# A transformer step whose second feed-forward runs its first w2 blocks as plain products, with earlier operand fetches and a norm in whole pieces

## The chip, the cores and the metric

The kernel runs on one NeuronCore of a Trainium2 chip. The metric is the device time of one execution in microseconds (us). Five engines work side by side: TensorE (PE, matrix products), VectorE (DVE), ScalarE (ACT), GpSimd (POOL) and SyncE (SP). SP and POOL issue most of the DMAs here, each from a queue of its own that goes out in order.

## The reference

One layer of a diffusion trunk on 640 tokens (512 latent, 128 context), width 1024: a SwiGLU feed-forward at half weight, token mixing (attention beside an mLSTM), and a second feed-forward at half weight. The part that is changed most is the second feed-forward, with the norm ahead of it:

```python
def swiglu(h, w1, w3, w2):
    return (jax.nn.silu(h @ w1) * (h @ w3)) @ w2
...
    hh = rmsnorm(x, g[2]) * (1 + m[7]) + m[6]
    x = x + 0.5 * m[8] * swiglu(hh, p['ffn2_w1'][l], p['ffn2_w3'][l], p['ffn2_w2'][l])
```

w1 and w3 are 1024 x 2816, w2 is 2816 x 1024. m[6] to m[8] are shift, scale and gate from the conditioning vector, one column per feature and kind of token.

## The kernel before

**Precision.** Each fp32 operand is held as a high part (rounded to fp32r) and a low part (the rest, also fp32r), and each product is three matmuls: high by high, high by low, low by high. To split something is therefore an ACT copy into the high part, and a DVE subtract for the low part. Weights that are split whole are called ww (a pair of 128x2048 tiles); those of some products come in smaller tiles wB and wC.

**Layout.** Features lie on partitions, tokens on the free axis; tokens come in two halves (hf) of 320, features of x in 8 tiles of 128 (KT), two of them to a pair. A matmul is 128x128 weights by 128x320.

**Up.** The 2816 hidden features are 11 blocks (FB) of 256. Block 0 is computed plainly from W, by 8 steps over k for the two output tiles f and both of w1, w3 (`plain`, L312). For each of the other ten blocks a granule (`Granule`, L230) holds 256 columns of w1, and another those of w3. Its product (2 x 2 in output tiles and token halves, two halves of the inner axis) goes through a scheme of Strassen's kind with seven products instead of eight: A11, S1, S2, A12, S3, A22, S4 (`products`, L378). The A are plain parts of the operands, the S sums of parts. For the weights, `parts` (L243) copies and splits the parts A11, A12 (wB) and S4 (wC), and then forms the sums in place in the raw tile; `sums` (L261) splits these into ww. For the tokens, `operand_sums` (L328) forms S1, S3, S2, S4 from the normed x, with a high part by ACT and a low part by DVE, into tiles S and hm. A granule's own A22 and S4 products (`tail`) run a granule later, between the next one's.

**Between.** silu and product give four quarters of a block in tile SO; `gated_sums` (L358) adds the four sums for down's scheme, and `store_g` (L346) splits 7 pieces into tiles g and writes them to g_dram on SP's queue.

**Down.** In the second half-step (`run`, L539) the 11 blocks form the groups 0-2, 3-6 and 7-10. For each group and each of four column blocks (j) of 256 outputs, a granule of w2 goes through the same seven products, with operands fetched from g_dram into the tiles of earlier operands (`fetch`, L553, on POOL's queue): each fetch is issued when TensorE has ended the last product that reads its tile, in the last granule before the group. In the first half-step (`run_whole`, L487) all groups of down are plain products with weights split whole (`Whole`, L270).

**Norm.** `normed` (L1774) takes one half of the tokens: for each feature tile and kind of token, DVE multiplies x by scale and 1/rms in one operation (L42), ACT writes the high part with the shift as its bias (L1788), DVE makes the low part. A pass on ACT later adds the shift to x itself (L1820), which the operand sums read. For the second half, the pieces are 192 and 128 tokens wide, since it holds latent and context tokens.

**Order.** TensorE and the loads (`dma`) keep the program's order. On the other engines and for the rest of SP's queue a list scheduler sets the order at build time from modelled times; `issue_after(ins)` ties what follows behind an instruction on the same engine.

Of the kernel before, what the change touches and what calls it, by code (L numbers as in the profile page):

```python
# [7 lines left out]
F32 = mybir.dt.float32  # L8
# [10 lines left out]
NS = 512  # L19
# [12 lines left out]
def tile_trunk(ctx: ExitStack, tc: tile.TileContext, a: dict):  # L32
# [197 lines left out]
    class Granule:  # L230
# [5 lines left out]
        def load(self):  # L236
            self.raw = rawp.tile([128, 2048], F32, tag="raw", name="raw")[:, : 512 * self.nk].rearrange("p (k n) -> p k n", n=256)
            self.fetch(self.raw)
# [22 lines left out]
        def sums(self):  # L261
# [4 lines left out]
            tt(vec, t[1], flat, t[0].bitcast(F32), ALU.subtract)  # L266
# [26 lines left out]
    class HalfStep:  # L293
        def __init__(self, n, fp, tmp, psum, w1, w3, w2, whole=False):

            self.whole, self.n_g = whole, 4 if whole else 8
            self.Q = {(kh, hf): kh + 2 * hf for kh in range(2) for hf in range(2)} if whole else Q
# [4 lines left out]
            self.g_dram = dp.tile([4 if whole else 7, 128, 2, FB, HALF], F32, name=f"g_dram{n}")  # L302
# [14 lines left out]
        def begin_gated(self):  # L317
            self.SO = self.fp.tile([128, 8, HALF], F32, tag="SO", name="SO")[:, : self.n_g]
# [9 lines left out]
        def operand_sums(self, pair):  # L328
# [6 lines left out]
            for i, to, x, y, op in (  # L335
                (S1, (1, 1), (0, 1), (1, 1), ALU.add), (S3, (0, 1), (0, 0), (0, 1), ALU.subtract),
                (S2, (0, 0), (1, 1), (0, 0), ALU.subtract), (S4, (1, 0), (1, 0), (0, 0), ALU.subtract),
            ):
                for r in range(2):
                    v, x_, y_ = (a[r][kh][hf] for kh, hf in (to, x, y))  # L340
                    ks = slice(2 * r, 2 * r + 2)
                    tt(vec, v, x_, y_, op)
                    act(SS[i][:, 0, ks], v, AF.Copy)
                    tt(vec, SS[i][:, 1, ks], v, SS[i][:, 0, ks].bitcast(F32), ALU.subtract)

        def store_g(self, SO, b):  # L346

            if not self.whole:
                self.gated_sums(SO)
            for tag, c0, c1 in (("gA", 0, 4), ("gB", 4, 7)):  # L350
                if c0 < self.n_g:
# [26 lines left out]
        def products(self, work, between, then=(), behind=None):  # L378
# [72 lines left out]
        def up_done(self, b):  # L451
# [10 lines left out]
            def of_w3(f, hf, p, u):  # L462
                if (f, hf) == (0, 0):
                    self.begin_gated()
# [9 lines left out]
        def fetch_w2(self, b0, b1, j):  # L474
            def f(raw):
                n = b1 - b0
                for h in range(2):
                    dma(raw[:, h * n : (h + 1) * n], self.w2[b0:b1, :, h, 256 * j : 256 * j + 256].rearrange("b p n -> p b n"))
# [60 lines left out]
        def run(self, x, gate, final, between, emptied=lambda: None, behind=None):  # L539


            work = self.up_work()

            at = {(0, i): self.ops[i] for i in range(7)}
            moves = {}
            for q, places in ((1, (None, None, 0, 1, 2, 3, 4)), (2, ((0, 5), 0, 1, (0, 6), 3, 4, 2))):
                for i, j in enumerate(places):
                    if j is not None:
                        before = j if type(j) is tuple else (q - 1, j)
                        at[q, i] = at.get(before)  # L550
                        moves[before] = q, i

            def fetch(q, i):  # L553
                b0, b1 = GROUPS[q]
# [1402 lines left out]
```

## Time and profile before

| | before |
|---|---|
| median of 3 runs | 1887.62 us (1882.26 to 1888.84) |
| profiled execution | 1888.76 us |
| its span | 1886.9 us |
| mean granted TensorE clock | 0.984 |
| DVE, ACT busy | 70%, 45% of the span |

A row of the timeline gives start, duration, engine, line, operation, output<-inputs, shapes and count, and in brackets how long the engine had been idle before and what ended it. A list of waits gives the total, the number and the longest. A row of a table of windows gives the window, then for PE, PEld, DVE, ACT and POOL busy us and count, then the granted clock, the share in which the DMA engines were busy, and GB/s. A group of instructions has its count, busy us, mean ns of one, and the idle time before it. A row on DMA issues has the count, KB of each and the median us from issue to landing. In the span the first half-step's feed-forward begins at about 40 us, the second's at 1443, its down part at 1730.

### The profile page before, as it was taken

The page shows a single profiled execution, that of the slowest core. Times are in us where ns is not written, and L with a number is a line of the kernel's source. Part 1 is how long each engine was busy: PE and PEld are TensorE (multiplying, and loading weights), DVE is VectorE, ACT ScalarE, POOL GpSimd, SP SyncE. Part 2 cuts the span into 40 slices and gives each one's busy share as a digit, 9 for nine tenths or more (in the row PEclk, how much of TensorE's full clock was granted, in tenths as well). Part 3 has the DMA queues.
Part 4 walks back from the last instruction along what each step waited for, and adds up shares of the span by engine and source line. Part 5 has one row for each costly group of instructions (what it writes and reads, how often), then busy time and mean ns, then how long its engine had stood idle before and what let it go on. Part 6 is the DMA issues. An engine that isn't in the chain of part 4 may idle for free.

```text
span 1886.9 us, 30810 instructions
## 1 busy us (share of the span) xinstructions
PE 1812.6 (96%) x12622; PEld 1774.3 (94%) x12622; DVE 1329.4 (70%) x2252; ACT 854.6 (45%) x1469; POOL 45.9 (2%) x71
## 2 busy tenths in 40 slices
PE   5899999999999999999999989999999999998989
PEld 4899999999999999999999979999999899998989
DVE  6888896577885675865755447864458888886775
ACT  5554444112454354543554445564325555553332
POOL 1000001010000000000000000000000000001100
PEclk8899999999999999999999999999999999999999
DMA  8344557964413323322222255564532455457962
GB/s 326 105 151 173 186 175 267 374 206 140 137 63 129 121 74 104 111 95 84 95 84 75 72 174 157 190 245 145 198 114 77 172 187 187 172 180 271 355 219 91
DMA packets 129614, 305.72 MB, mean 162 GB/s; under 512 B 9601, under 2 KB 93057, under 8 KB 116673
## 3 DMA queue, kind: packets, MB, share of 16 engines
q1 hardware_dynamic: 117298, 247.33, 38.1%
q0 software_dynamic: 12176, 56.43, 7.9%
q8 instruction: 99, 1.62, 0.4%
q14 instruction: 41, 0.34, 0.1%
HBM read 237.15 MB, written 66.58 MB: 161 GB/s over the span
## 4 chain that ended last, share of the span: by engine, by line
PE 82%; DVE 8%; DMA 6%; ACT 2%; issue 1%; SPq 0%; DVEq 0%; ACTq 0%
PE ps_f L52 36%; PE ps_p L52 22%; PE ps_t L52 12%; PE sc L52 2%; PE ps_o L52 2%; PE ps_n L52 2%; DMA raw<-in_w2b 2%; DMA ada<-csil_dram 2%; DVE ww L39 1%; PE ps_u L52 1%; PE ps_wT L55 1%; PE ps_qkT L55 1%; DVE x L42 1%; DVE raw L39 1%; DMA raw_a<-in_w_ada_c 0%
## 5 line engine op out<-in xcount | busy, mean ns | idle before, releaser
L52 PE MATMUL ps_f<-S,ww 128*128 128x320 f32 x2052 | 332.2, 311 | 5.6 <-DVE S L39 4.2
L52 PEld LDWEIGHTS ps_f<-S,ww 128*128 128x128 f32 x2052 | 309.9, 189 | 8.3 <-DVE S L39 4.7
L52 PE MATMUL ps_p<-hH,wH 128*128 128x320 f32 x864 | 274.1, 317 | 3.3 <-ACT aT L1275 2.5
L52 PE MATMUL ps_p<-hH,wL 128*128 128x320 f32 x864 | 267.5, 310 | 0.0
L52 PE MATMUL ps_p<-hL,wH 128*128 128x320 f32 x864 | 267.3, 309 | 0.0
L52 PE MATMUL ps_t<-wH,hH 128*128 128x256 f32 x640 | 186.3, 291 | 1.0 <-DVE x L42 1.0
L52 PE MATMUL ps_f<-hm,wB 128*128 128x320 f32 x1128 | 182.5, 311 | 0.0
L52 PE MATMUL ps_t<-wH,hL 128*128 128x256 f32 x640 | 182.4, 285 | 0.0
L52 PE MATMUL ps_t<-wL,hH 128*128 128x256 f32 x640 | 182.1, 285 | 0.0
L52 PEld LDWEIGHTS ps_f<-hm,wB 128*128 128x128 f32 x1128 | 170.9, 189 | 0.0
L52 PE MATMUL ps_f<-hm,ww 128*128 128x320 f32 x996 | 158.0, 311 | 11.7 <-ACT u L375 9.5
L52 PEld LDWEIGHTS ps_p<-hH,wH 128*128 128x128 f32 x864 | 162.9, 189 | 4.8 <-ACT aT L1275 2.7
L39 DVE TENSOR_TENSOR ww<-raw,ww 128x2048 fp32r<-128x2048 f32 (+1 forms) x62 | 138.7, 2237 | 35.6 <-ACT ww L265 23.4
L52 PEld LDWEIGHTS ps_p<-hL,wH 128*128 128x128 f32 x864 | 163.0, 189 | 0.5
L52 PEld LDWEIGHTS ps_p<-hH,wL 128*128 128x128 f32 x864 | 162.6, 188 | 0.0
L52 PEld LDWEIGHTS ps_f<-hm,ww 128*128 128x128 f32 x996 | 149.8, 189 | 12.5 <-ACT u L375 10.1
L39 DVE TENSOR_TENSOR wL<-raw,wH 128x2048 fp32r<-128x2048 f32 x49 | 112.1, 2289 | 40.0 <-ACT wH L123 39.9
L39 DVE TENSOR_TENSOR raw<-raw 128x1024 f32<-128x1024 f32 (+2 forms) x156 | 132.7, 851 | 2.1
L123 ACT ACTIVATE wH<-raw 128x2048 fp32r<-128x2048 f32 x49 | 93.6, 1911 | 87.5 <-PE ps_p L52 83.3
L265 ACT ACTIVATE ww<-raw 128x2048 fp32r<-128x2048 f32 (+1 forms) x52 | 97.8, 1880 | 73.2 <-PE ps_f L52 51.7
L52 PEld LDWEIGHTS ps_t<-wH,hH 128*128 128x128 f32 x640 | 123.7, 193 | 2.0 <-issue 1.2
L52 PEld LDWEIGHTS ps_t<-wH,hL 128*128 128x128 f32 x640 | 123.7, 193 | 0.5 <-DVE hL L42 0.5
(294 smaller groups left out, 3288.1 us busy)
## 6 DMA issues: line engine op xcount, KB each, us to landing
g_dram<-g SPq DMA_DIRECT2D x44, 640.0 KB, 4.2
raw_a<-in_w_ada_c SPq DMA_DIRECT2D x24, 512.0 KB, 4.1
hm<-g_dram POOLq DMA_DIRECT2D x9, 1280.0 KB, 12.9
raw<-in_w1b SPq DMA_DIRECT2D x11, 1024.0 KB, 4.8
raw<-in_w3b SPq DMA_DIRECT2D x11, 1024.0 KB, 4.8
g_dram<-g SPq DMA_DIRECT2D x22, 480.0 KB, 4.6
raw<-in_w1a SPq DMA_DIRECT2D x10, 1024.0 KB, 4.9
raw<-in_w3a SPq DMA_DIRECT2D x10, 1024.0 KB, 5.9
```

The source lines that it names most:

```text
L39: return eng.tensor_tensor(out=out, in0=in0, in1=in1, op=op)
L42: return vec.scalar_tensor_tensor(out=out, in0=in0, scalar=scalar, in1=in1, op0=op0, op1=op1)
L52: tc.keep_in_program_order(nc.tensor.matmul(*args, **kw))
L55: tc.keep_in_program_order(nc.tensor.transpose(*args, **kw))
L123: act(h, raw, AF.Copy)
L265: act(t[0], flat, AF.Copy)
```

## The change

Four parts of the program are changed.

1. Down's first group of the second half-step (blocks 0-2) becomes plain: no gated sums for these blocks, four stored pieces, weights split whole.
2. Its operands are fetched on SP's queue as the last up granule ends with each of A11, S1, S2, A12; those of the second group during the plain stage, placed behind weight loads; two of the third group's on SP behind the load of the second group's last granule, the other five on POOL in that granule.
3. The norm multiplies by 1/rms in DVE operations over a pair of tiles, ACT applies scale and shift twice (into the high part L1838 and into x itself L1839), and the low part is one DVE subtract a pair. The shift pass is gone.
4. The operand sums stand in an order written out by hand, and a granule's parts are tied behind the split of the granule before it (of the first granule in the second half-step: behind the low part of S2). `products` and `operand_sums` serve both half-steps.

```diff
-    GROUPS = ((0, 3), (3, 7), (7, FB))
+    GROUPS = ((3, 7), (7, FB))
+    PLAIN_Q = {(kh, hf): kh + 2 * hf for kh in range(2) for hf in range(2)}
...
-            tt(vec, t[1], flat, t[0].bitcast(F32), ALU.subtract)
+            self.split_at = tt(vec, t[1], flat, t[0].bitcast(F32), ALU.subtract).ins
...
-        def begin_gated(self):
-            self.SO = self.fp.tile([128, 8, HALF], F32, tag="SO", name="SO")[:, : self.n_g]
+        def begin_gated(self, b):
+            self.Q, n = (PLAIN_Q, 4) if b < self.n_plain else (Q, 8)
+            self.SO = self.fp.tile([128, 8, HALF], F32, tag="SO", name="SO")[:, :n]
...
+            for f, i, r in (
+                (terms, S1, 0), (terms, S1, 1), (terms, S3, 0), (low, S1, 0), (terms, S2, 0), (low, S1, 1), (terms, S3, 1),
+                (terms, S2, 1), (low, S2, 0), (low, S2, 1), (low, S3, 0), (low, S3, 1), (terms, S4, 0), (terms, S4, 1),
             ):
-                for r in range(2):
-                    v, x_, y_ = (a[r][kh][hf] for kh, hf in (to, x, y))
-                    ks = slice(2 * r, 2 * r + 2)
-                    tt(vec, v, x_, y_, op)
-                    act(SS[i][:, 0, ks], v, AF.Copy)
-                    tt(vec, SS[i][:, 1, ks], v, SS[i][:, 0, ks].bitcast(F32), ALU.subtract)
+                f(i, r)
+                if (f, i) == (low, S2):
+                    behind = prev.ins
+            low(S4, 0)
+            low(S4, 1)
+            return behind
 
         def store_g(self, SO, b):
 
-            if not self.whole:
+            n = 4
+            if b >= self.n_plain:
                 self.gated_sums(SO)
+                n = 7
...
-            work[0][0].parts(self.fp)
-            work[0][0].sums()
+            if not prepared:
+                work[0][0].parts(self.fp)
+                work[0][0].sums()
...
                 if not last:
-                    with ExitStack() as st:
-                        if i == 0 and behind is not None:
-                            st.enter_context(tc.issue_after(behind))
+                    with tc.issue_after(behind if i == 0 and behind is not None else gr.split_at):
                         work[i + 1][0].parts(self.fp)
...
-        def run(self, x, gate, final, between, emptied=lambda: None, behind=None):
+        def run(self, x, gate, final, behind=None):
...
+            n = self.n_plain
+            down = [Whole(n, self.fetch_w2(0, n, j)) for j in range(4)]
+
+            up = self.ops
+            at = [[up[i] for i in (A11, S1, S2, A12)], [up[i] for i in (S3, S4, A22)], None]
+
+            def fetch(q, i, eng=nc.sync):
+                b0, b1 = ((0, n), *GROUPS)[q]
+                eng.dma_start(out=at[q][i][:, :, : b1 - b0].bitcast(F32), in_=self.g_dram[i, :, :, b0:b1, :])
...
-            def fetch(q, i):
-                b0, b1 = GROUPS[q]
-                nc.gpsimd.dma_start(out=at[q, i][:, :, : b1 - b0].bitcast(F32), in_=self.g_dram[i, :, :, b0:b1, :])
...
+            work[-1][3] = lambda i: {A11: lambda: fetch(0, 0), S1: lambda: fetch(0, 1), S2: lambda: fetch(0, 2), A12: lambda: fetch(0, 3)}.get(i, nothing)()
+            self.products(work, nothing, down[:2], behind=behind)
+            at[1] += [self.fp.tile([128, 2, 4, HALF], F32R, tag=tag, name="op") for tag in ("gA", "SO")] + at[0][:2]
...
                 def used(i):
-                    if j == 3 and (q, i) in moves:
-                        fetch(*moves[q, i])
+                    if q == 1 and j == 3 and i in moves:
+                        fetch(2, moves[i], nc.gpsimd)
...
+            moves = {A11: S2, S1: A12, S2: S3, A12: A22, S3: S4}
+            for j in range(4):
+                ahead = down[j + 2] if j < 2 else last[j - 2][0]
+                loaded = ahead.load()
+                with tc.issue_after(loaded):
+                    for i in ((A11, S1), (S2, A12), (S3,), ())[j]:
+                        fetch(1, i)
+                if j < 3:
+                    down[j + 1].split()
+                else:
+                    last[0][0].parts(self.fp)
+                    last[0][0].sums()
+                for hf in range(2):
+                    for f in range(2):
+                        p = acc_tile(self.psum)
+                        for kh in range(2):
+                            op = at[0][PLAIN_Q[kh, hf]]
+                            for b in range(n):
+                                w = [down[j].w(i, n * kh + b, f) for i in range(2)]
+                                mm3(p, *w, op[:, 0, b], op[:, 1, b], kh + b == 0, kh == 1 and b == n - 1)
+                        add_residual(x, p, 2 * j + f, hf, gate)
+                    if (j, hf) == (3, 0):
+                        for i in (A22, S4):
+                            fetch(1, i, nc.gpsimd)
+
+            def load_last(load=last[3][0].load):
+                with tc.issue_after(load()):
+                    for i in (A11, S1):
+                        fetch(2, i)
+
+            last[3][0].load = load_last
+            self.products(last, nothing, prepared=True)
...
-        for d in range(KT):
-            for s0, s1, j in SEGS[hf]:
-                xs = x[d][:, s0:s1]
-                h, lo = (t[:, s0 - c0 : s1 - c0] for t in hs.hh(d, hf))
-                sh = shift[:, d, j : j + 1]
-                stt(xs, xs, scale[:, 2, d, j : j + 1], rs[:, s0 - c0 : s1 - c0], ALU.mult, ALU.mult)
-                act(h, xs, AF.Identity, bias=sh)
-                ins = stt(lo, xs, sh, h.bitcast(F32), ALU.add, ALU.subtract)
-        return ins.ins
+        for g in range(4):
+            xs = x_pairs[g][:, :, half(hf)]
+            tt(vec, xs, xs, rs[:, None, :].to_broadcast([128, 2, HALF]), ALU.mult)
+            for d in (2 * g, 2 * g + 1):
+                for s0, s1, j in SEGS[hf]:
+                    by = dict(scale=scale[:, 2, d, j : j + 1], bias=shift[:, d, j : j + 1])
+                    act(hs.hh(d, hf)[0][:, s0 - c0 : s1 - c0], x[d][:, s0:s1], AF.Identity, **by)
+                    act(x[d][:, s0:s1], x[d][:, s0:s1], AF.Identity, **by)
+            p = hs.part[g // 2, hf][:, :, 2 * (g % 2) : 2 * (g % 2) + 2]
+            tt(vec, p[:, 1], xs, p[:, 0].bitcast(F32), ALU.subtract)
...
-    for d in range(KT):
-        for s0, s1, j in ((0, NS, 0), (NS, T, 1)):
-            xs = x[d][:, s0:s1]
-            act(xs, xs, AF.Identity, bias=m_of(6)[:, d, j : j + 1])
-    hs.operand_sums(lambda r: x_pairs[r])
+    summed = hs.operand_sums(lambda r: x_pairs[r])
```

What this does to the order. First, TensorE where down begins; hm and S are operand tiles, ww, wB, wC weights. Before, one column block of the group:

```order
L52 MATMUL ps_f<-hm,wB 128x320 x9
L52 MATMUL ps_f<-S,ww 128x320 x9
L52 MATMUL ps_f<-hm,ww 128x320 x9
L52 MATMUL ps_f<-S,ww 128x320 x9
L52 MATMUL ps_f<-hm,wC 128x320 x9
L52 MATMUL ps_f<-hm,wB 128x320 x9
L52 MATMUL ps_f<-S,ww 128x320 x9
```

and now, where the rows of one column block are 9, 9, 9, 18, 9, 9 and 9 with the last and first of neighbours joined:

```order
L52 MATMUL ps_f<-hm,ww 128x320 x18
L52 MATMUL ps_f<-S,ww 128x320 x9
L52 MATMUL ps_f<-hm,ww 128x320 x9
L52 MATMUL ps_f<-S,ww 128x320 x18
L52 MATMUL ps_f<-hm,ww 128x320 x9
L52 MATMUL ps_f<-S,ww 128x320 x9
```

A column block has 72 matmuls instead of 63, all with whole split weights, on four operands instead of seven.

Second, SP's queue at the same place, from the first loads of w2 on (L74; raw is a weight tile, hm, S and op are operand tiles). Before:

```order
L74 DMA raw<-in_w2b 128x3x256 x4
L356 DMA g_dram_14354<-g 128x4x320
L356 DMA g_dram_14354<-g 128x3x320
L356 DMA g_dram_14354<-g 128x4x320
L356 DMA g_dram_14354<-g 128x3x320
L74 DMA raw<-in_w2b 128x3x256 x4
L356 DMA g_dram_14354<-g 128x4x320
L356 DMA g_dram_14354<-g 128x3x320
L356 DMA g_dram_14354<-g 128x4x320
L356 DMA g_dram_14354<-g 128x3x320
L74 DMA raw<-in_w2b 128x4x256 x16
```

and now, from behind the first loads and two stores:

```order
L581 DMA hm<-g_dram_14354 128x2x960
L384 DMA g_dram_14354<-g 128x4x320
L384 DMA g_dram_14354<-g 128x3x320
L581 DMA S<-g_dram_14354 128x2x960 x2
L74 DMA raw<-in_w2b 128x3x256 x2
L581 DMA hm<-g_dram_14354 128x2x960
L581 DMA S<-g_dram_14354 128x2x1280
L581 DMA hm<-g_dram_14354 128x2x1280
L384 DMA g_dram_14354<-g 128x4x320
L74 DMA raw<-in_w2b 128x3x256 x2
L581 DMA hm<-g_dram_14354 128x2x1280
```

The fetches (L581), which were all on POOL's queue, now stand between the loads and the stores. POOL keeps seven of 128x2x1280.

Third, ACT at the norm of the second half of the tokens (s is the silu of block 0). Before, the end of the norm and the shift pass:

```order
L1788 ACTIVATE hm<-x,mod 128x128
L1788 ACTIVATE hm<-x,mod 128x192
L1820 ACTIVATE x<-x,mod 128x512
L1788 ACTIVATE hm<-x,mod 128x128
L1820 ACTIVATE x<-x,mod 128x128
L1820 ACTIVATE x<-x,mod 128x512
L1820 ACTIVATE x<-x,mod 128x128
L325 ACT_TABLE_LOAD
L325 ACTIVATE s<-ps_f 128x320
```

and now:

```order
L1839 ACTIVATE x<-x,mod,scale 128x192
L1839 ACTIVATE x<-x,mod,scale 128x128
L1838 ACTIVATE hm<-x,mod,scale 128x128
L1839 ACTIVATE x<-x,mod,scale 128x192
L327 ACT_TABLE_LOAD
L327 ACTIVATE s<-ps_f 128x320
L1839 ACTIVATE x<-x,mod,scale 128x128
L1839 ACTIVATE x<-x,mod,scale 128x192
L1839 ACTIVATE x<-x,mod,scale 128x128
L327 ACTIVATE s<-ps_f 128x320
```

The last operations on x, which the low parts of the last two pairs now read, stand behind the table load and a silu.

Fourth, DVE amid the first half-step's norm (mod, small and scale belong to the modulation). Before, with the second granule's parts (wB, wC, raw) among the norm's pieces:

```order
L42 SCALAR_TENSOR_TENSOR scale<-mod,g_norm 128x2
L39 TENSOR_TENSOR wB<-raw,wB 128x1024
L39 TENSOR_TENSOR raw<-raw 128x4x128
L39 TENSOR_TENSOR wC<-raw,wC 128x512
L42 SCALAR_TENSOR_TENSOR x<-x,scale,ry 128x320
```

and these parts now, behind the split ww of the first granule:

```order
L39 TENSOR_TENSOR ww<-raw,ww 128x2048
L39 TENSOR_TENSOR wB<-raw,wB 128x1024
L39 TENSOR_TENSOR wC<-raw,wC 128x512
L39 TENSOR_TENSOR S<-x,S 128x640
```

They have moved past the rest of the norm and most of the operand sums.

More of the change, by code (lines that the diff above doesn't have):

```diff
@@ new lines, in operand_sums, with next_of_vec, terms @@
+            prev = None
+            def next_of_vec(*args):
+                nonlocal prev
+                with ExitStack() as st:
+                    if prev is not None:
+                        st.enter_context(tc.issue_after(prev.ins))
+                    prev = tt(vec, *args)
+            def terms(i, r):
+                to, x_, y_, op = places[i]
+                v, x_, y_ = (a[r][kh][hf] for kh, hf in (to, x_, y_))
+                next_of_vec(v, x_, y_, op)
+                act(SS[i][:, 0, 2 * r : 2 * r + 2], v, AF.Copy)
@@ L376, in copy_of, with products @@
             return t
-        def products(self, work, between, then=(), behind=None):
+        def products(self, work, between, then=(), behind=None, prepared=False):
             n = len(work)
@@ L1826, in tile_trunk @@
         lambda: x, half_m[:, 1], lambda d, hf: nc.sync.dma_start(out=a["y"][:, d, half(hf)], in_=x[d][:, half(hf)]),
[L1827 removed]
+        behind=summed,
     )
```

75 lines of the change are left out of this document (31 added, 44 removed).

## The prediction

> **What bounds the kernel now.** I read the page's first lines, then TensorE's list of waits, then its timeline around each long wait.
>
> ```profile
> span 1886.9 us, 30810 instructions
> ...
> PE 1812.6 (96%) x12622; PEld 1774.3 (94%) x12622; DVE 1329.4 (70%) x2252; ACT 854.6 (45%) x1469; POOL 45.9 (2%) x71
> ```
>
> TensorE is busy for 1812.6 of 1886.9 us. So only two things move the time: the number of matmuls, and the 74.3 us in which TensorE is idle, with the slow stretches behind them. The waits from 1250 us on, which hold the second half-step:
>
> ```profile
> PE ps_f L52 <- ACT u L375: 8.1, 1, 8.1
> PE ps_f L52 <- ACT ww L265: 4.6, 1, 4.6
> PE ps_f L52 <- DVE S L39: 4.2, 2, 2.9
> ...
> PE ps_f L52 <- DMA S<-g_dram: 0.7, 1, 0.7
> ```
>
> They lie at three places, and TensorE's timeline shows each (start, duration, count, idle time before).
>
> ```profile
> 1474.78 2.07 PE L52 MATMUL ps_f<-S,ww 128*128 128x320 f32 x13
> 1478.14 1.15 PE L52 MATMUL ps_f<-S,ww 128*128 128x320 f32 x6 [1.29 <-DVE S L39]
> 1482.21 1.70 PE L52 MATMUL ps_f<-S,ww 128*128 128x320 f32 x5 [2.93 <-DVE S L39]
> 1483.71 3.40 PE L52 MATMUL ps_f<-hm,wB 128*128 128x320 f32 x12
> 1486.91 2.40 PE L52 MATMUL ps_f<-S,ww 128*128 128x320 f32 x12
> 1489.14 1.92 PE L52 MATMUL ps_f<-hm,wB 128*128 128x320 f32 x12
> 1490.90 1.33 PE L52 MATMUL ps_f<-S,ww 128*128 128x320 f32 x8
> ...
> 1735.70 1.48 PE L52 MATMUL ps_f<-S,ww 128*128 128x320 f32 x9
> 1745.25 2.77 PE L52 MATMUL ps_f<-hm,ww 128*128 128x320 f32 x9 [8.07 <-ACT u L375]
> 1747.82 2.60 PE L52 MATMUL ps_f<-S,ww 128*128 128x320 f32 x9
> 1750.22 1.74 PE L52 MATMUL ps_f<-hm,wC 128*128 128x320 f32 x9
> 1751.79 1.48 PE L52 MATMUL ps_f<-hm,wB 128*128 128x320 f32 x9
> ...
> 1796.67 2.31 PE L52 MATMUL ps_f<-op,wB 128*128 128x320 f32 x12
> 1803.59 0.90 PE L52 MATMUL ps_f<-op,ww 128*128 128x320 f32 x2 [4.60 <-ACT ww L265]
> 1805.91 3.03 PE L52 MATMUL ps_f<-op,ww 128*128 128x320 f32 x10 [1.42 <-DVE ww L39]
> 1808.74 3.42 PE L52 MATMUL ps_f<-hm,ww 128*128 128x320 f32 x22
> ```
>
> Undisturbed, 12 matmuls take 1490.90 - 1489.14 = 1.76 us, 0.1467 us each. After a long idle time they run at about half of that speed: 12 in 1486.91 - 1483.71 = 3.20 us. A stall thus costs more than its wait. **A** (the start of the weight products, waiting for operand sums): 48 matmuls are worth 7.04 us and took 1489.14 - 1474.78 = 14.36, so 7.3 lost. **B** (from up to down): 36 matmuls, worth 5.28, took 1751.79 - 1735.70 = 16.09, so 10.8, and 0.7 for the operand that was late just before: 11.5 lost. **C** (from the second down group to the third): 24, worth 3.52, took 12.07: 8.55 lost.
>
> ACT's timeline names the cause of B and C.
>
> ```profile
> 1740.43 0.52 ACT L250 ACTIVATE wC<-raw 128x384 fp32r<-128x384 f32 x1 [10.72 <-DMA raw<-in_w2b]
> ...
> 1794.89 1.06 ACT L250 ACTIVATE wB<-raw 128x1024 fp32r<-128x1024 f32 x1 [2.85 <-DMA raw<-in_w2b]
> ```
>
> In B, ACT stands 10.72 us at a weight part whose load is late; the copy u, which TensorE waits for (8.07), is queued behind it. In C the late load delays the weight parts and so the split. The loads are late because seven operand fetches were issued just ahead (DMA share and GB/s are the last two columns):
>
> ```profile
> 1725.00:1740.00 15.00, 11.51 (x77) 11.01 (x76) 4.94 (x9) 2.07 (x3) 1.43 (x2) 1.00 1.04 398
> ...
> 1750.00:1800.00 50.00, 48.86 (x329) 48.33 (x328) 37.82 (x62) 18.64 (x27) 5.64 (x8) 0.99 0.88 327
> ```
>
> The DMA engines are full in the first of these stretches.
>
> **Part 1, the plain group.** Seven products become eight: per column block 72 matmuls for 63, four blocks, 36 more. 36 x 0.1467 = **+5.3 us**, certain, since TensorE is the bound. What goes with it (the four sums of SO and three of seven stored pieces, for each of two blocks) lies on DVE and SP beside TensorE, and I count it at nothing.
>
> **Part 2, the fetches.** Call T the start of the last up granule. The first group's four operands (960 KB each) are now issued at T+1.8, 3.5, 7.0 and 10.6, as TensorE finishes with A11, S1, S2 and A12 (a product is 12 matmuls), and are wanted from T+15.8 to T+22.4.
>
> ```profile
> hm<-g_dram POOLq DMA_DIRECT2D x4, 960.0 KB, 7.8
> hm<-g_dram POOLq DMA_DIRECT2D x4, 1280.0 KB, 12.0
> ```
>
> At the 7.8 us of before's rush they land in time, the last by 4 us. No weight part on ACT waits at this border now: down's first two blocks are loaded before T, and a plain block needs one ACT copy and one DVE subtract of 1536 columns in a stage of 72 x 0.1467 = 10.6 us. So nothing holds the copy u, and B goes: **-11.5**. The next group's operands are wanted only after four such stages (42.2 us, T+58); in the queue's order the fetches and loads go out between T+12 and T+53. By about T+60 it must move 4 x 0.98 MB, 5 x 1.31, two 0.79 MB blocks for the plain stage, two of 1.05 MB and 2.3 MB of stores, 16.4 MB: 273 GB/s. The 327 above clears that. The slack is thin at one place: the split of the next group's second block, which I get at T+67.9 for T+68.6. The third group's five fetches of 1280 KB on POOL (12.0 us) now stand behind weight loads that SP issued before, and are wanted 16 to 19 us after issue, so C goes too: **-8.55**. Each of these two terms could also be nothing, if a load stays late.
>
> **Part 3, the norm, at A.** For the second half of the tokens, DVE's 32 operations become 8 of 640 columns; ACT's 16, and the 16 of the shift pass, become 32 that carry a scale and a bias. TensorE waited for none of this before; now a pair's low part waits for all of its ACT operations, which stand 16th, 23rd, 30th and 35th (the last two behind a table load).
>
> ```profile
> 1451.72 4.94 ACT L1788 ACTIVATE hm<-x,mod 128x192 fp32r<-128x192 f32 x15 [2.06 <-DVE x L42]
> ...
> 1458.78 1.28 ACT L325 ACT_TABLE_LOAD   x1
> ...
> L181 ACT ACTIVATE nsq<-x 128x320 f32<-128x320 f32 x42 | 19.2, 467 | 38.4 <-DVE x L42 36.8 <-DVE nacc L39 0.7
> L1788 ACT ACTIVATE hm<-x,mod 128x320 fp32r<-128x320 f32 x8 | 3.8, 549 | 1.3 <-DVE x L42 1.3
> ```
>
> One such operation takes 4.94/15 = 0.33 us with one column operand (the bias). Such an operand costs 549 - 467 = 82 ns (without and with, same size). A second isn't shown in this trace. Its bounds are nothing and twice that; I take a like amount, rounded up, so 0.42 us. The first starts at 1452.1 (1451.72, and DVE's piece ahead of it is 0.4 longer), the 16th ends at 1452.1 + 16 x 0.42 = 1458.8, and its low part 0.8 later, about 0.95 us after TensorE wants it; the next three come 2.0, 3.0 and 1.3 late: 7.2, and some 3.4 of half speed, by the dip above. The 96 matmuls of this half, begun at 1458.75, end at 1483.4 instead of 1473.0. But A's own waits, which came from sums being late, are over by then: six products later S1 of the second granule begins at 1494.0 (before: 1490.90). With the second operand free the norm's waits are about 4 and S1 comes 1 to 2 us earlier than before. Between -2 and +3.1 I take **+1.5**.
>
> The Trainium skill, page "ScalarE: Activation LUTs", section "What ACT_TABLE_LOAD costs", says that each [128,1] pointer operand adds about 93 ns to an ACTIVATE. The rows for one operand agree (82 ns); no run here shows two. By it the 32 operations cost 3.0 us more, and the sum would stand at the upper end of my bounds, about 1874.
>
> **Part 4, the order at the first half-step's start.** The second granule's weight parts, on DVE amid the norm, move behind the first granule's split.
>
> ```profile
> 45.74 1.22 DVE L39 TENSOR_TENSOR wB<-raw,wB 128x1024 fp32r<-128x1024 f32 x1
> ...
> 66.24 1.14 DVE L42 SCALAR_TENSOR_TENSOR hm<-x,mod,hm 128x320 fp32r<-128x320 f32 x3
> ...
> L39 DVE TENSOR_TENSOR S<-x,S 128x640 fp32r<-128x640 f32 x12 | 9.7, 818 | 0.1
> L39 DVE TENSOR_TENSOR ww<-raw,ww 128x2048 fp32r<-128x2048 f32 x56 | 128.2, 2289 | 27.3 <-ACT ww L265 18.6 <-ACT ww L283 8.6
> ...
> 64.42 13.98 PE L52 MATMUL ps_f<-hm,wH 128*128 128x320 f32 x83 [2.15 <-DVE hm L42]
> 78.23 1.92 PE L52 MATMUL ps_f<-hm,wB 128*128 128x320 f32 x12
> ...
> 92.18 2.02 PE L52 MATMUL ps_f<-hm,ww 128*128 128x320 f32 x12 [1.47 <-ACT u L375]
> ```
>
> With the norm alone on DVE its last piece ends 4.7 us earlier, at 62.7 instead of 67.4, and without the slow stretch behind the waits the plain units end near 68.2 instead of 78.2, 10.0 earlier. What is late next is the second granule's split. Ahead of it and with it DVE has 15 sums and low parts (0.74 each back to back, 0.08 under the row's mean), two splits (4.5), one set of parts (4.0), the split of g (1.5) and five operations of 320 columns (2.0): 23.1 us, to 85.8. TensorE would want it at 79.2; with what it waits for first that is 6.2 us, and up to 3.4 of half speed. Against that goes the wait of 1.47 at 92.18 with its dip, 1.7 in all. So between -5.5 and 0; I take **-3**. In the steady stretch the same tie leaves a granule's parts (4.0 us of DVE) the 10.5 us from its predecessor's S1 to its own A11, and costs nothing.
>
> **Sum.** 5.3 - 11.5 - 8.55 + 1.5 - 3 = -16.3. The profiled execution took 1888.76 us (span 1886.9), the median of the runs is 1887.62; from the former, **1872**.
>
> **Rivals.**
> - *The stall moves to the new border.* The fetches sit in SP's one queue with the weight loads and wait there for TensorE to free their tiles; loads behind them go late, and the split at T+67.9 has only 0.7 us to lose. With B's price at that place: 1872.5 + 11.5 = 1884. For it: 10.72 us on such a load before. Against: two column blocks are ahead. The Trainium skill, "DMA: Bandwidth & Descriptors", section "Issuing engines are not separate DMA queues", speaks for it: changing the queue buys no bandwidth. The share of 1.04 above agrees; only issuing earlier can help.
> - *The norm binds on ACT* with low parts later than my 0.42 us gives, and half speed through most of the 96 matmuls: another 3.4 twice over, 1879.
> - *A clears as well*: second operand free, sums in time: 5.3 - 7.3 - 11.5 - 8.55 - 3 = -25, so 1864.
> - *The plain group is bound by its transfers* (slower).
>
> ```profile
> DMA packets 129614, 305.72 MB, mean 162 GB/s; under 512 B 9601, under 2 KB 93057, under 8 KB 116673
> ```
>
> At this mean 16.4 MB take 101 us where 60 are to be had: 41 us of wait and a dip of 3.4, so 1917. It ends slower below about 190 GB/s (86 us); 327 and 398 in the stretches shown above speak against it.
>
> **How the numbers follow.** Forecast 0.55 (about 1866 to 1878), moved stall 0.14, ACT-bound norm 0.12, A clears 0.12, transfers 0.07. The range 1861 to 1884 leaves out the transfers, half of the moved stall and the low edge of the clearing case. A measurement of this kernel tells about 0.5% from no change, 9.4 us: faster (below 1878) 0.73: the forecast, A clearing and half of the ACT case; same 0.20: the moved stall and the other half; slower 0.07.
>
> **What would show it.** TensorE's wait list loses ACT u 8.1 and ACT ww 4.6, and the plain group's 288 matmuls follow at 0.147 us each. Waits of 1 to 3 us on DVE hm appear in the 96 matmuls of the second half of the tokens, and DVE S 4.2 goes. ACT's norm operations show 0.40 to 0.45 us spacing. The first half-step's units end near 68. A wait on DMA op or S, or on ww near the plain group's end, would make the forecast wrong, as would hm waits over 10 us.

## The result, and the profile after

The changed kernel takes 1870.65 us (median of 4 runs, 1868.95 to 1874.16), the kernel before 1887.08 (4 runs): a ratio of 0.9919, 95% interval 0.9894 to 0.9944. The profiled execution took 1874.16 us. The page of the changed kernel, its first two lines of numbers:

```profile
span 1872.4 us, 30753 instructions
...
PE 1812.7 (97%) x12658; PEld 1774.4 (95%) x12658; DVE 1300.2 (69%) x2177; ACT 849.6 (45%) x1455; POOL 35.8 (2%) x57
```

TensorE has 36 instructions more (12658 for 12622) and is busy as long, so, by estimate, some 5 us at half speed went as the extra 36 came in; the rest of what went is idle time, 14.6 us of it (74.3 to 59.7). TensorE's list of waits from 1250 us on, where before had ACT u 8.1, ACT ww 4.6 and DVE S 4.2:

```profile
PE ps_f L52 <- DVE hm L39: 4.4, 2, 2.6
PE ps_p L52 <- DVE y L39: 0.7, 1, 0.7
PE ps_ss L52 <- ACT nsq L181: 0.2, 1, 0.2
```

Only one long kind of wait is left, and it is a new one: the low parts of the norm. TensorE's timeline at the norm (A), and where down begins (B):

```profile
1462.67 0.41 PE L52 MATMUL ps_f<-hm,wH 128*128 128x320 f32 x1 [1.77 <-DVE hm L39]
...
1466.44 0.63 PE L52 MATMUL ps_f<-hm,wH 128*128 128x320 f32 x1 [2.63 <-DVE hm L39]
...
1481.20 1.92 PE L52 MATMUL ps_f<-hm,wB 128*128 128x320 f32 x12
...
1491.76 2.17 PE L52 MATMUL ps_f<-S,ww 128*128 128x320 f32 x12
...
1497.29 1.92 PE L52 MATMUL ps_f<-hm,wC 128*128 128x320 f32 x12
...
1712.01 1.92 PE L52 MATMUL ps_f<-hm,wB 128*128 128x320 f32 x12
...
1726.09 3.24 PE L52 MATMUL ps_f<-hm,ww 128*128 128x320 f32 x21
...
1768.81 1.48 PE L52 MATMUL ps_f<-hm,ww 128*128 128x320 f32 x9
1770.13 1.92 PE L52 MATMUL ps_f<-S,wB 128*128 128x320 f32 x12
1771.89 3.68 PE L52 MATMUL ps_f<-hm,ww 128*128 128x320 f32 x24
...
1780.69 5.44 PE L52 MATMUL ps_f<-hm,ww 128*128 128x320 f32 x36
```

From 1712.01 (the last up granule) to the end no row has an idle time in brackets: the plain group, 1727.8 to 1770.1, runs its 288 matmuls at 0.147 us each, and both borders behind it pass. The margin is small. DVE's timeline has the two splits that TensorE wants at 1771.89 and 1780.69:

```profile
1768.29 2.28 DVE L39 TENSOR_TENSOR ww<-raw,ww 128x2048 fp32r<-128x2048 f32 x1
...
1777.88 2.29 DVE L39 TENSOR_TENSOR ww<-raw,ww 128x2048 fp32r<-128x2048 f32 x1
```

They end 1.3 and 0.5 us ahead of need. At the border into the plain group (B) ACT waits for TensorE now, and no longer for a load; its timeline there, with the copy u that was held up before:

```profile
1724.59 0.44 ACT L403 ACTIVATE u<-ps_f 128x320 f32<-128x320 f32 x1 [2.58 <-PE ps_f L52]
1727.90 1.49 ACT L285 ACTIVATE ww<-raw 128x1536 fp32r<-128x1536 f32 x1 [2.88 <-PE ps_f L52]
```

But the operands have no margin left there: the plain group's last one was issued at 1722.3, landed 12.0 us later at 1734.34, and is wanted at 1734.45. In e12, a second profile of the same kernel, TensorE waits for it (its timeline):

```profile
1733.60 1.59 PE L52 MATMUL ps_f<-hm,ww 128*128 128x320 f32 x9 [0.59 <-DMA hm<-g_dram]
```

e1, e3, e4, e8 and e10 have the same wait, of 0.3 to 1.1 us. The DMA engines were full meanwhile (windows of the changed kernel; share and GB/s last):

```profile
1727.00:1742.00 15.00, 15.00 (x104) 14.96 (x104) 10.83 (x17) 5.26 (x4) 0.00 (x0) 1.00 1.04 398
1742.00:1757.00 15.00, 15.00 (x104) 15.00 (x104) 4.97 (x9) 2.81 (x3) 0.00 (x0) 1.00 1.04 378
```

At the first half-step's start, TensorE's timeline:

```profile
68.59 1.92 PE L52 MATMUL ps_f<-hm,wB 128*128 128x320 f32 x12
...
84.27 0.90 PE L52 MATMUL ps_f<-S,ww 128*128 128x320 f32 x2 [4.22 <-ACT ww L267]
86.60 3.04 PE L52 MATMUL ps_f<-S,ww 128*128 128x320 f32 x10 [1.42 <-DVE ww L39]
...
94.36 1.92 PE L52 MATMUL ps_f<-hm,wC 128*128 128x320 f32 x12
```

The plain units (the matmuls of block 0) end 9.6 us earlier than before (68.59 for 78.23), and the wait that takes their place is that of the second granule's split.

To see what each place is worth, the span is cut at three matmuls that all the kernels have: the first wC product of either half-step (94.36 and 1497.29 above), and the first plain matmul of the second half-step. In the kernel before these are

```profile
95.80 1.92 PE L52 MATMUL ps_f<-hm,wC 128*128 128x320 f32 x12
...
1443.78 0.46 PE L52 MATMUL ps_f<-hm,wH 128*128 128x320 f32 x2
...
1496.18 1.92 PE L52 MATMUL ps_f<-hm,wC 128*128 128x320 f32 x12
```

I is the first half-step's start, II all from there to the second half-step (it holds the first half-step's later granules, where the ties of edit 4 act too; the rest of its code is the same everywhere but for moves by the scheduler), III the norm, sums and first granule of the second half-step, IV the rest, with both borders. Each row is one profile; the medians are of the timed runs. The e-runs come from three chips (e1, e2, e4, e5; e3, e6, e7, e8; e10 to e13), on which the kernel before took 1886.1, 1887.2 and 1887.4 us.

| kernel | I | II | III | IV | span | median |
|---|---|---|---|---|---|---|
| before | 95.8 | 1348.0 | 52.4 | 390.7 | 1886.9 | 1887.1 |
| changed | 94.4 | 1349.4 | 53.5 | 375.1 | 1872.4 | 1870.7 |
| e12 (changed, again) | 92.4 | 1349.9 | 53.3 | 375.9 | 1871.6 | 1873.4 |
| e1 norm of before | 92.0 | 1346.3 | 53.6 | 375.7 | 1867.6 | 1871.7 |
| e2 x on DVE | 92.3 | 1351.1 | 52.6 | 375.0 | 1871.0 | 1872.6 |
| e7 x on DVE, second half | 93.1 | 1349.6 | 53.1 | 375.5 | 1871.2 | 1870.6 |
| e8 and S4 behind | 93.6 | 1349.1 | 47.8 | 376.3 | 1866.8 | 1868.1 |
| e3 no ties | 87.5 | 1349.0 | 59.6 | 376.7 | 1872.7 | 1875.3 |
| e11 first tie off | 90.3 | 1347.7 | 57.1 | 375.1 | 1870.2 | 1872.4 |
| e10 e8, first tie off | 90.0 | 1350.2 | 47.8 | 376.5 | 1864.4 | 1863.4 |
| e4 late second group | 93.0 | 1348.9 | 53.3 | 382.9 | 1878.1 | 1878.4 |
| e5 all on POOL | 93.3 | 1349.1 | 53.3 | 382.7 | 1878.4 | 1881.3 |
| e6 third group's two early | 92.1 | 1345.1 | 53.7 | 382.3 | 1873.1 | 1876.9 |
| e13 third group's two late | 93.6 | 1350.5 | 53.5 | 383.3 | 1880.9 | 1878.8 |

The gain is in IV: 15.6 us there, 1.4 in I, less 1.1 in III and 1.4 in II. II runs from 1345.1 to 1351.1 over these profiles (e6 and e2, whose edits lie elsewhere), which is the measure of how far one profile's total can be trusted; I, III and IV of like code agree within 2.3, 0.4 and 1.6.

### The profile page after: what moved, and what is told of

Read it like the earlier page. It is cut to its first block, busy times and chain, and to the rows that moved or that the text cites. A ratio compares the mean times of both kernels' runs of the same rounds, so it can differ in the third digit from the quotient of the medians.

```text
span 1872.4 us, 30753 instructions
## 1 busy us (share of the span) xinstructions
PE 1812.7 (97%) x12658; PEld 1774.4 (95%) x12658; DVE 1300.2 (69%) x2177; ACT 849.6 (45%) x1455; POOL 35.8 (2%) x57
## 4 chain that ended last, share of the span: by engine, by line
PE 86%; DVE 7%; DMA 4%; ACT 2%; issue 1%; SPq 0%; DVEq 0%; ACTq 0%
PE ps_f L52 41%; PE ps_p L52 22%; PE ps_t L52 12%; PE ps_o L52 2%; PE sc L52 2%; PE ps_n L52 2%; PE ps_u L52 1%; DMA ada<-csil_dram 1%; PE ps_wT L55 1%; DVE ww L39 1%; PE ps_qkT L55 1%; DMA P<-nm_dram 1%; DMA so<-o_dram 0%; DVE wL L39 0%; DMA raw_a<-in_w_ada_c 0%
## 5 line engine op out<-in xcount | busy, mean ns | idle before, releaser
L52 PE MATMUL ps_f<-S,ww 128*128 128x320 f32 x1992 | 322.9, 311 | 6.7 <-ACT ww L267 4.2
L52 PEld LDWEIGHTS ps_f<-S,ww 128*128 128x128 f32 x1992 | 301.1, 189 | 9.7 <-ACT ww L267 4.5
L52 PE MATMUL ps_f<-hm,ww 128*128 128x320 f32 x1248 | 198.2, 311 | 2.0 <-DVE ww L39 2.0
L52 PEld LDWEIGHTS ps_f<-hm,ww 128*128 128x128 f32 x1248 | 188.2, 190 | 2.3 <-DVE ww L39 2.2
L52 PE MATMUL ps_f<-hm,wB 128*128 128x320 f32 x1008 | 161.5, 309 | 0.0
L52 PEld LDWEIGHTS ps_f<-hm,wB 128*128 128x128 f32 x1008 | 151.3, 188 | 0.0
L123 ACT ACTIVATE wH<-raw 128x2048 fp32r<-128x2048 f32 x49 | 93.6, 1911 | 89.4 <-PE ps_p L52 85.5
L39 DVE TENSOR_TENSOR raw<-raw 128x1024 f32<-128x1024 f32 x144 | 124.6, 865 | 1.9
L52 PEld LDWEIGHTS ps_t<-wL,hH 128*128 128x128 f32 x640 | 123.3, 193 | 0.2
```

What stands on the lines that cost most here:

```text
L39: return eng.tensor_tensor(out=out, in0=in0, in1=in1, op=op)
L52: tc.keep_in_program_order(nc.tensor.matmul(*args, **kw))
L123: act(h, raw, AF.Copy)
```

## The experiments

Each is the changed kernel with one edit.

**The norm: e1, e2, e7, e8.** e1 takes the norm and the shift pass of before:

```diff
-            tt(vec, xs, xs, rs[:, None, :].to_broadcast([128, 2, HALF]), ALU.mult)
...
+                stt(xs, xs, scale[:, 2, d, j : j + 1], rs[:, s0 - c0 : s1 - c0], ALU.mult, ALU.mult)
+                act(h, xs, AF.Identity, bias=sh)
+                ins = stt(lo, xs, sh, h.bitcast(F32), ALU.add, ALU.subtract)
```

> The norm of before and its shift pass, all else as changed. My theory (the norm in whole pieces moves the waits from the operand sums to the low parts and comes out about even): no hm waits in the second half of the tokens, its 96 matmuls end near 1473 instead of 1481.2, DVE S waits return, and S1 of the second granule begins near 1489.5 (changed kernel 1491.8, before 1490.9); total about 1868 to 1871. Rival (the norm edit is worth its own gain): S1 of the second granule at 1494 or later, total 1874 or more.

Total 1871.68 us (1869.39 to 1873.88), ratio to before 0.9929 (0.9911 to 0.9948); stretch III 53.6. So the edit to the norm is worth nothing either way, as expected, though the waits on S that were expected back did not come. What was not expected is the place of the loss either. TensorE's timeline of e1:

```profile
1468.07 1.92 PE L52 MATMUL ps_f<-hm,wB 128*128 128x320 f32 x12
...
1482.95 0.90 PE L52 MATMUL ps_f<-S,ww 128*128 128x320 f32 x2 [4.16 <-ACT ww L267]
1485.28 3.03 PE L52 MATMUL ps_f<-S,ww 128*128 128x320 f32 x10 [1.42 <-DVE ww L39]
```

No wait on S returns (the sums' new order serves them in time); the second granule's split is what TensorE waits for now, and it loses there what it won at the hm waits. e2 keeps the new norm but gives x's scale and shift to DVE, e7 does so for the second half of the tokens alone:

```diff
-                    act(x[d][:, s0:s1], x[d][:, s0:s1], AF.Identity, **by)
+                    ts(x[d][:, s0:s1], x[d][:, s0:s1], by["scale"], ALU.mult, by["bias"], ALU.add)
```

> The changed kernel, with the scale and shift of x itself given to DVE as one operation with two column operands, so that ACT has 16 instead of 32 such operations per half. Theory (the low parts wait for ACT's operations with two column operands, 0.42 us each): the hm waits of 1.8 and 2.6 us shrink to 1 or less, the 96 matmuls end near 1474 instead of 1481.2, S1 of the second granule near 1486, total some 5 us less, about 1865. Rival (the sums on DVE set the time whatever the norm does): S1 of the second granule stays at 1490 to 1492 and the total at 1870 to 1871.

> As e2_x_on_dve, but only for the second half of the tokens; for the first ACT keeps both operations. Theory (DVE's operations for the first half delayed the sum of squares, 2.8 us of wait, and hid the gain): no wait on DVE nacc there, the 96 matmuls end near 1474 for a start at 1443.8, and what is late next is the second granule's split, so that the stretch from the start of the second half-step to its first wC takes 50 to 52.5 us (changed kernel 53.5); total 1867 to 1870. Rival: the stretch stays at 53 or more.

e2: 1872.64 us, III 52.6, not 5 us less: here the rival was nearer. TensorE waits 2.8 us there for the sum of squares (nacc), which DVE now reaches later. e7: 1870.57 us, III 53.1, so by its own bounds its rival holds too. In e7 the hm waits are gone and the plain units end at 1472.79 for a start at 1442.69, as the theory had it, yet (TensorE's timeline):

```profile
1485.89 0.56 PE L52 MATMUL ps_f<-S,ww 128*128 128x320 f32 x2 [2.38 <-ACT ww L267]
1488.22 3.03 PE L52 MATMUL ps_f<-S,ww 128*128 128x320 f32 x10 [1.77 <-DVE ww L39]
```

7.3 us won at the norm (37.4 to 30.1 from start to the units' end), all but 0.5 lost at the split. e8 tests what holds the split: it moves the sums of S4, the reload of x and the store of block 0 behind it.

```diff
                     work[i + 1][0].sums()
+                    if i == 0 and after_split is not None:
+                        after_split(work[1][0])
```

> e7_x_dve_second with the sums of S4 (and the reload of x and the store of block 0) moved behind the second granule's split on DVE, in the second half-step only. Theory (after the norm is off ACT, DVE's row up to that split sets the time, and S4 is not wanted before it): the stretch from the start of the second half-step to its first wC takes 46 to 49 us instead of 53.5, total 1863 to 1867. Rival (something else, ACT or the raw tile, holds the split): the stretch at 50 or more, total as e7.

III falls to 47.8, as the theory said. What is left of the wait, in e8's TensorE timeline:

```profile
1485.39 1.73 PE L52 MATMUL ps_f<-S,ww 128*128 128x320 f32 x10 [1.64 <-DVE ww L39]
```

The total, 1868.11 us (1863.92 to 1872.66), ratio 0.9903 (0.9871 to 0.9934), is above the 1863 to 1867 of the theory and can't be told from e7's 1870.57 (1865.51 to 1872.96); the gain is shown in the stretch alone. So the norm on ACT and DVE's row up to the second split are two limits of nearly the same length. Taking away the first alone showed nothing (e1, e7). The second alone was not run; but in the changed kernel TensorE has no idle time from 1481.20 to 1497.29, so an earlier split could win it next to nothing there. Which of the three moves in e8 counts is not separated.

**The tie: e3, e11, e10.** e3 drops the ties of a granule's parts behind the split before it (all but the one behind the sums of the second half-step), e11 only the first one of the first half-step, e10 adds e11's edit to e8. The edit of e11:

```diff
-                    with tc.issue_after(behind if i == 0 and behind is not None else gr.split_at):
+                    with ExitStack() as st:
+                        if i or behind is not None:
+                            st.enter_context(tc.issue_after(behind if i == 0 else gr.split_at))
```

> The changed kernel without the ties of a granule's parts behind the split before it (the one behind the operand sums of the second half-step stays). Theory (the tie moves the second granule's parts off the first norm and gives a few us there): the first half-step's plain units end 5 to 10 us later than the 67 to 69 of the runs with the tie, its first wC product 1 to 4 us later than their 92 to 94.4, and the total 1 to 4 us more, 1871 to 1875. Rival (a wait later in the token mixing takes the gain back, as the trace of the changed kernel can be read): the second half-step begins when it does with the tie, total within 1 of it.

> The changed kernel with only that tie taken away. Theory: first wC at 87 to 89 instead of 92 to 94.4, the second half-step's stretch as in the changed kernel (53 to 54, where the fully untied run had 59.6), total 2 to 5 under the changed kernel beside it. Rival (what the untied run lost lay in the first half-step's later granules): the stretch at 53 to 54, but total as the changed kernel or above.

> e8_s4_behind with the tie of the second granule's parts taken away in the first half-step alone (the untied run had its first wC product at 87.5 us there, the tied ones at 92.0 to 94.4). Theory (the tie costs at the first half-step and pays in the second): first wC at 87 to 89, the second half-step's stretch still 46 to 49, total 1860 to 1866, 3 to 6 under the changed kernel run beside it less what the token mixing takes back. Rival: the mixing takes all of it back, total as e8, 1866 to 1870.

My theory for e3 fell: the units end later without the tie, as it said (71.6), but the first wC product comes at 87.5 and not later than 92.0 to 94.4. Without the tie the second granule's split is ready and TensorE never waits for it:

```profile
71.63 1.92 PE L52 MATMUL ps_f<-hm,wB 128*128 128x320 f32 x12
...
82.19 1.92 PE L52 MATMUL ps_f<-S,ww 128*128 128x320 f32 x12
...
87.47 1.92 PE L52 MATMUL ps_f<-hm,wC 128*128 128x320 f32 x12
```

So stretch I's gain over before comes from the hand order of the sums, by elimination the one edit that is left in it, and the ties take part of it back. In the second half-step e3 loses: its III is 59.6, 6 longer. e11 keeps the later ties, and wins 2 to 4 in I (90.3 for the tied 92.0 to 94.4, not the 87 to 89 expected), but its III is 57.1, which neither its theory nor its rival had: the list scheduler puts a weight part wB and a silu ahead of the second split on ACT there, presumably because its modelled times shifted. ACT's timeline of e11:

```profile
1481.98 1.06 ACT L252 ACTIVATE wB<-raw 128x1024 fp32r<-128x1024 f32 x1 [1.18 <-PE ps_f L52]
1482.95 0.42 ACT L489 ACTIVATE s<-ps_f 128x320 f32<-128x320 f32 x1
...
1484.22 1.90 ACT L267 ACTIVATE ww<-raw 128x2048 fp32r<-128x2048 f32 x1
```

In the changed kernel that split precedes wB (1487.92 and 1489.73). e3 has that order on ACT as well, so only 2.4 of its 6 us are more than e11 loses with those ties in place. The total of e11, 1872.36 (1869.66 to 1875.47), can't be told from that of the changed kernel beside it, 1873.37 (1871.93 to 1875.47), for which this was expected:

> The changed kernel itself, beside the others on their chip: 1868 to 1874; in its profile the first wC at 92 to 94.5, the second half-step's stretch 53 to 54, the rest 375 to 376.

In e10, S4's explicit place keeps III at 47.8, and I is 90.0: **1863.41 us** (1859.99 to 1866.79), ratio to before 0.9864 (0.9845 to 0.9882), 10 us under the changed kernel on the same chip by the medians, 7.2 by the two profiles, and the fastest of all. Total and III are as expected; the first wC, at 90.0, is later than the 87 to 89.

**The fetches: e4, e5, e6, e13.** e4 fetches five of the second group's operands in the plain group's last column block:

```diff
-                    for i in ((A11, S1), (S2, A12), (S3,), ())[j]:
+                    for i in ((), (), (), (A11, S1, S2, A12, S3))[j]:
```

> The changed kernel, but the five operands of the second down group that went out from SP one or two column blocks early are all fetched in the plain group's last column block, as before fetched a group's operands in the last granule ahead of it. Theory (issuing early is what closes the border): a wait on DMA hm or S, or on the split behind a late load, of 3 to 9 us at the plain group's end and half speed behind it, total 1876 to 1883. Rival (the plain group alone closes the border, the transfers would be hidden anyway): no wait there, total 1870 to 1872.

1878.42 us (1874.94 to 1879.89), IV 7.8 longer than in the changed kernel, at the border where the theory put it (TensorE's timeline):

```profile
1775.44 2.03 PE L52 MATMUL ps_f<-op,wB 128*128 128x320 f32 x12 [1.46 <-DMA op<-g_dram]
1780.96 3.26 PE L52 MATMUL ps_f<-op,ww 128*128 128x320 f32 x12 [3.49 <-DMA op<-g_dram]
```

The plain group alone does not close the border; issuing early does. e5 puts all fetches on POOL's queue at the same places:

```diff
-            def fetch(q, i, eng=nc.sync):
+            def fetch(q, i, eng=None):
+                eng = nc.gpsimd
```

> The changed kernel with all operand fetches of the second half-step on POOL's queue, at the same places of the program, free of the ties behind the weight loads. Theory (when a fetch goes out matters, not on which queue): no new wait over 1 us, total 1869 to 1873. Rival (SP's order, loads ahead of fetches, protects the loads): the split of the second group's second block, with 0.6 us to spare, is late by several us, total 1875 to 1882.

The rival holds in size: 1881.25 us, IV 7.6 longer. ACT's timeline shows weight loads arriving late, since nothing holds the fetches behind them now:

```profile
1740.27 1.49 ACT L285 ACTIVATE ww<-raw 128x1536 fp32r<-128x1536 f32 x1 [8.90 <-DMA raw<-in_w2b]
1748.82 1.49 ACT L285 ACTIVATE ww<-raw 128x1536 fp32r<-128x1536 f32 x1 [7.05 <-DMA raw<-in_w2b]
1755.71 1.06 ACT L252 ACTIVATE wB<-raw 128x1024 fp32r<-128x1024 f32 x1 [5.41 <-DMA raw<-in_w2b]
...
1782.31 1.06 ACT L252 ACTIVATE wB<-raw 128x1024 fp32r<-128x1024 f32 x1 [1.37 <-DMA raw<-in_w2b]
```

The first three rows lie in the plain group, and TensorE waits 1.0 us for ww at its end. The place of its long wait is not the second block of the second group, as the rival had it, but the third, whose load the last row waits for:

```profile
1795.13 0.56 PE L52 MATMUL ps_f<-hm,ww 128*128 128x320 f32 x2 [2.32 <-ACT ww L267]
1797.45 6.79 PE L52 MATMUL ps_f<-hm,ww 128*128 128x320 f32 x34 [1.77 <-DVE ww L39]
```

That load was issued at 1772.10, after the third group's first two fetches (POOL, 1767.6 and 1768.9), which in this run are free to go early, and landed 10.1 us later (5.4 in the changed kernel). e6 below has those two early fetches alone, with a wait at the same block. The bytes are the same on either queue; the order against the loads is not. (The scheduler, told of later loads, also placed DVE's wB later, so the loads' lateness and its echo in the order are not separated.) e6 and e13 move the third group's A11 and S1 from behind the second group's last load into that granule:

```diff
-            moves = {A11: S2, S1: A12, S2: S3, A12: A22, S3: S4}
+            moves = {A11: (A11, S2), S1: (S1, A12), S2: (S3,), A12: (A22,), S3: (S4,)}
```

> The changed kernel, but the third group's A11 and S1 go out on POOL in the second group's last granule with the other five, as all seven did before. Theory (C came from weight loads issued into that rush; now the loads are ahead of it, so seven fetches there do little): no wait over 1.5 us at that border, total 1869 to 1873. Rival (the two early fetches are what closes C): a wait of 2 to 5 us on DMA or on ww there, total 1875 to 1880.

In e6 the scheduler let the two go at once on POOL, their tiles being free. The changed kernel issues them on SP at 1781.2 and 1781.8; its down part runs 6.5 us later in the span than e6's, so e6 is 11 to 12 us earlier. POOL's timeline, and the wait on TensorE's:

```profile
1762.81 0.70 POOL L581 DMA_DIRECT2D S<-g_dram  x1 [3.25 <-PE ps_f L52]
1764.13 0.71 POOL L581 DMA_DIRECT2D hm<-g_dram  x1 [0.62 <-DVE ww L39]
```

```profile
1789.60 0.90 PE L52 MATMUL ps_f<-hm,ww 128*128 128x320 f32 x2 [2.89 <-ACT ww L267]
```

The wait is at the third block of the second group, as in e5, and not at the border where the theory looked. The load behind the two, in two pieces, landed 12.4 and 13.5 us after its issue (4.4 and 5.4 in the changed kernel). So e6 does not test lateness; it shows that two fetches ahead of a weight load cost as much (IV 7.2 longer, 1876.90 us). e13 ties them behind the first of the five:

> The changed kernel with all seven operands of the third group fetched on POOL in the second group's last granule, the two that the change takes out of there tied behind the first of the five (in e6_late_third they went out ahead instead, at 1762.8 and 1764.1). Theory (C came from the rush of seven fetches into which a weight load falls): a weight load of the third group lands some 6 us later, a wait on ww of 2 to 5 us and half speed behind it in the third group, the stretch from the second half-step's first wC to the end 379 to 384 instead of 375 to 376, total 1874 to 1880. Rival (the loads are far enough ahead now): 375 to 377, total as the changed kernel.

TensorE's timeline of e13:

```profile
1823.49 6.21 PE L52 MATMUL ps_f<-hm,ww 128*128 128x320 f32 x24 [5.29 <-DMA hm<-g_dram]
```

1878.84 us, IV 8.2 longer, as the theory's size said, and a weight load does land 6 us later as well (19.4 us after its issue for 13.3). But what TensorE waits for is not that load but an operand of the rush itself: S1, one of the two that moved, issued at 1808.64 and landed at 1823.45.

## Why the prediction was right

- **Sum.** 16.3 was forecast off the profiled execution, 1872 in all. The medians moved by 16.4, the spans by 14.5: the profiled execution of the changed kernel, 1874.16, is the slowest of its four, and stretch II, for which nothing was forecast, is 1.4 longer in it.
- **Parts 1 and 2.** 5.3 - 11.5 - 8.55 = -14.75 was forecast for what is stretch IV; measured -15.6, and -14.8 in e12. The 36 matmuls are there. The tight split, put at T+67.9 for T+68.6, is at T+68.2 for T+68.7 (T = 1712.01). That placing the fetches closed C is shown by e13, which brings back 8.2 us at that border; e4, e5 and e6 (7.8, 7.6 and 7.2) show that without the other placings the second group would have stalled. No run undoes B, the largest term: that it went, with ACT's wait for a load, is read from the trace, and what closes it (plain with four operands, or the loads ahead of T) was not tried apart. With seven products all seven tiles are in use, and the second group can't be fetched early. One step there was mis-sized: the fetches of the first group were to land in 7.8 us, the last 4 us ahead of need. They took 7.5, 10.8, 10.9 and 12.0 us, and the last came 0.1 us ahead of need, 0.6 behind it in e12. That B went whole is to this extent luck.
- **Part 3.** +1.5 forecast, +1.1 and +0.9 measured. An ACT operation with two column operands takes 0.41 us back to back, 0.42 assumed: four of them, of 192 and 128 columns, from 1454.24 to 1455.89 in ACT's timeline of the changed kernel.

```profile
1454.24 1.75 ACT L1838 ACTIVATE hm<-x,mod,scale 128x192 fp32r<-128x192 f32 x4
1455.89 0.92 ACT L1839 ACTIVATE x<-x,mod,scale 128x128 f32<-128x128 f32 x2
```

   The waits on hm were over-sized: 1.8 and 2.6 against 0.95, 2.0, 3.0 and 1.3, so the 96 matmuls end at 1481.2 and not 1483.4. That the price came out right is luck: e1, with the old norm, has the same stretch (53.6), so the new norm by itself costs nothing. The second granule's split stands close behind it, as e7 and e8 show, and takes back what the old norm would save; the working has no such limit in it.
- **Part 4.** -3 forecast, -1.4 and -3.4 measured; ten profiles with the tie have -1.4 to -3.8. The units' end (68.59; 68.2 forecast) and the late split (4.2 + 1.4; 6.2 forecast) are as worked out. But I had put the gain down to the parts' move, and that step was wrong: e3 has a larger gain without it, 8.3, and of the edits only the hand order of the sums is left there. The parts' move brings the end of the units forward (68.59 for e3's 71.63), and loses more at the split that it makes late.
- **Rivals.** The stall did not move to the new border, where e4 shows it at 7.8 and not the 11.5 that I priced. The transfers ran at 378 to 398 GB/s in the first 30 us of the plain group, above the 273 needed. (The limit of about 190 GB/s in the last rival leaves out the dip of 3.4 that the line above it counts; with it the limit is nearer 200. Nothing hangs on it.) On the rule of the Trainium skill, "DMA: Bandwidth & Descriptors", section "Issuing engines are not separate DMA queues": e5 is in line with it, as another queue won nothing; but e5 also frees the fetches from their place behind the weight loads, and lost 7.6 us, and of such an order the rule says nothing.

## What to carry to other kernels

A long transfer should be issued by when it is wanted *and* behind the loads that are wanted sooner: e4 and e13 (late) and e5 and e6 (early, but ahead of loads) cost the same 7 to 8 us. A longer plain stage can be worth its 36 extra matmuls (5.3 us) where it goes with transfers that then find time, as here, where both were changed together. Where removing a wait changes nothing, look for a second limit of like length before calling the first harmless: in stretch III e7 won 0.5 us, the same edit with the next limit moved won 5.7.

## What the runs showed of the hardware

The groups of the changed kernel's ACT by shape show the second column operand, which no row of before had:

```profile
L1838 ACT ACTIVATE hm<-x,mod,scale 128x320 fp32r<-128x320 f32 x8 | 4.5, 648 | 0.0
```

648 ns, against 549 with one and 467 with none: 99 and 82 ns. The Trainium skill's 93 ns for each ("ScalarE: Activation LUTs", "What ACT_TABLE_LOAD costs") lies between them. The other rows with one operand of this size take 558 to 563 ns, so only the sum, 181 ns for both, is firm. Stretch II took between 1345 and 1351 us from profile to profile, both ends with the same code in it, as much as several of the edits moved.
